# A decoder layer step on one core: norms in steps beside the output projection, shared weight slots, GpSimd stores, outputs fed by the last products

## The chip, the core and the metric

The kernel runs on one core of a Trainium2 chip. TensorE (PE) multiplies, VectorE (DVE), ScalarE (ACT) and GpSimd (POOL) do the elementwise work, and SyncE (SP) issues most DMA transfers; each engine works through its own instructions in order, and a DMA queue through its transfers. The metric is the device time of one execution in microseconds (us).

## What is computed

One layer of a decoder for a prompt of 1024 tokens and 8 sample tokens, 1032 columns in all, with width 1024 and a hidden width of 2816 in both feed-forward networks (FFN):

```python
x = x + 0.5 * swiglu(rms_norm(x, g_ffn1), w1_gate, w1_up, w1_down)
h = rms_norm(x, g_mix)
proj = h @ w_in                     # S5 input, q, k, v, two gates
y_ssm, ... = s5_branch(...)
y_attn, kv_new = dilated_attention_branch(...)
mixed = gate_ssm * (y_ssm @ w_ssm_proj) + gate_attn * (y_attn @ w_attn_proj)
x = x + mixed @ w_o
x = x + 0.5 * swiglu(rms_norm(x, g_ffn2), w2_gate, w2_up, w2_down)
```

## The kernel before

**Arithmetic and tiles.** Every fp32 operand is split in a high part (an ACT cast) and a low part (a DVE subtraction of the cast), and a product is three matmuls: high by high, high by low, low by high. Activations lie with their features on the partitions and the tokens on the free axis, in three chunks of 344. Weights come as 512 KB loads of 128x1024 and are split like the rest.

**Stages.** First FFN (to about 815 us), the mixing stage (`mix`: input projection, S5, attention, gates, `ssm_proj`, to about 1529 us), then at the end of `mix` the join: `attn_proj` of chunks 0 and 1, `wo` of chunk 0, `attn_proj` of chunk 2, `wo` of chunks 1 and 2 (to about 1655 us). `attn_proj` (L1112) multiplies by the gate and adds the other branch; `wo` (L1127) is the output projection, added to the residual in `xT`. Then `wo_norm` (L1152) runs for each of the three chunks: it stores `xT` to the buffer `x_d` in device memory, sums squares (`ss`, L1164), multiplies (`xT`, L1169), and writes the operands of the second FFN (`put`, L1172), which needs sums and differences of chunk 0 and 1 (L1182 to L1187).

**Second FFN.** `ffn_up` (L1244) walks over 22 hidden tiles `f`. Chunks 0 and 1 go through Winograd's form of Strassen's scheme: seven products (`A11*B11`, `S2*T2`, `S3*T3`, `S1*T1`, `A12*B21`, `A22*T4`, `S4*B22`) of 12 matmuls each. Chunk 2 takes four direct ones (`D0`, `D1`) of 12. `wprep` prepares the weights of the next `f` a few steps ahead. `second` (L1262) forms the operands of the down projection from two tiles at a time, splits them into tiles `hs` and stores them to the buffer `hs_d` on SP's queue (55 stores, L1267). `ffn_down` (L1357) runs in three groups of 4, 4 and 3 pairs of hidden tiles. For each group it loads weights (`rd`), loads parts back from `hs_d` (`hload`, L1376), does nine products of four tiles (`run`, L1389, matmuls at L1396), and adds them to accumulators (L1403). In the last group the accumulators are combined (L1443 to L1482), and `out` (L1405) loads the residual `y` from `x_d`, adds it (L1409), transposes on PE (L1415), copies (L1416) and stores (L1420).

**Order and memory.** The order of each engine's instructions comes from the framework's scheduler. SBUF pools are opened and closed like a stack: a tile of a new pool waits for the last reader of what lay in its place. The weight pool `wp` is opened anew for the first FFN and for `mix`; the join uses `wp` too. The second FFN's weights have a pool `wq` of their own, and `ffn_down` has another, `wd`.

## Time and profile before

| | us |
|---|---|
| three timed runs | 2431.59, 2437.26, 2441.64 (median 2437.26) |
| the profiled execution | 2433.45, of which the span of instructions is 2431.7 |
| PE busy | 2308.2 (95%) |
| DVE busy | 1383.5 (57%) |
| ACT busy | 785.0 (32%) |
| POOL busy | 263.4 (11%) |
| mean granted TensorE clock | 0.973 of 2.4 GHz |

A row of the chain of waits is: start, length, engine, tile and line. A row of a table of windows is: the stretch, its length, then for each engine the busy time and (x) the instructions, the granted clock, the share of the DMA engines and GB/s. A row of a table of lines is: line, engine, operation, names, shapes, count, then busy us and mean ns, and idle time ahead with what ended it.

### The profile page before, as it was taken

What the parts mean: (1) busy time and instruction counts of PE and PEld (TensorE: products, weight loads), DVE (VectorE), ACT (ScalarE), POOL (GpSimd) and SP (SyncE); (2) the same over time, 40 slices, a digit from 0 to 9 for tenths busy, and PEclk for the clock granted to TensorE, in tenths of its full rate; (3) what the DMA queues carried; (4) which work ended last, traced back from release to release, by engine and by line L of the source; (5) the groups of instructions that cost most, each with busy time, mean ns of one, the idle gap of its engine ahead of it and who ended that gap; (6) DMA issues with size and microseconds to landing.
All of it is one profiled execution on the core that took longest, in us unless ns stands there. A gap on an engine that the chain in (4) does not pass through costs nothing.

```text
span 2431.7 us, 37109 instructions
## 1 busy us (share of the span) xinstructions
PE 2308.2 (95%) x14409; PEld 2209.9 (91%) x14409; DVE 1383.5 (57%) x2930; ACT 785.0 (32%) x1486; POOL 263.4 (11%) x808
## 2 busy tenths in 40 slices
PE   7999999999999899989999999895999999979996
PEld 6999999999999799978887888894999999979995
DVE  7656544455433734555574535778666666645365
ACT  6211111111112443555444432343333333323121
POOL 3057776000001200000000000000000000000000
PEclk8999999999999899999999999997999999989998
DMA  5333434323232577541331256662333343375453
GB/s 139 96 112 102 126 103 121 112 85 114 90 99 84 159 207 233 164 135 43 96 99 38 73 155 206 185 190 74 112 120 126 113 140 116 128 284 206 161 171 136
DMA packets 306998, 319.44 MB, mean 131 GB/s; under 512 B 30414, under 2 KB 262510, under 8 KB 304262
## 3 DMA queue, kind: packets, MB, share of 16 engines
q1 hardware_dynamic: 302470, 268.86, 35.3%
q10 hardware_dynamic: 2816, 44.00, 6.0%
q0 software_dynamic: 1536, 4.21, 0.5%
q8 instruction: 113, 1.85, 0.3%
q14 instruction: 63, 0.52, 0.1%
HBM read 241.42 MB, written 119.59 MB: 148 GB/s over the span
## 4 chain that ended last, share of the span: by engine, by line
PE 88%; DVE 6%; DMA 4%; ACT 1%; issue 1%; SPq 0%; ACTq 0%; DVEq 0%
PE pm L157 52%; PE pm L1241 18%; PE pm L1396 9%; PE ps L670 2%; PE acc L686 1%; DVE xn L128 1%; PE pT L679 1%; PE pn L969 1%; DMA raw<-in_w_in_dram 1%; DVE wl L143 1%; DMA xr<-in_x_prompt_dram 0%; DMA raw<-in_w_glu_dram 0%; PE pT L809 0%; PE pT L456 0%; DVE al L130 0%
## 5 line engine op out<-in xcount | busy, mean ns | idle before, releaser
L157 PE MATMUL pm<-al,wh 128*128 128x344 f32 x2224 | 709.8, 324 | 2.1 <-DVE rs L1122 1.4
L157 PE MATMUL pm<-ah,wh 128*128 128x344 f32 x2096 | 680.2, 325 | 3.9 <-ACT ah L129 1.9
L157 PE MATMUL pm<-ah,wl 128*128 128x344 f32 x2032 | 656.5, 323 | 0.0
L157 PEld LDWEIGHTS pm<-al,wh 128*128 128x128 f32 x2224 | 418.2, 189 | 10.7 <-issue 4.5
L157 PEld LDWEIGHTS pm<-ah,wh 128*128 128x128 f32 x2096 | 396.3, 189 | 14.6 <-issue 5.6
L157 PEld LDWEIGHTS pm<-ah,wl 128*128 128x128 f32 x2032 | 384.1, 189 | 7.1 <-issue 4.3
L142 ACT CAST wh<-raw 128x1024 fp32r<-128x1024 f32 (+1 forms) x154 | 152.0, 993 | 437.3 <-PE pm L157 384.2
L143 DVE TENSOR_TENSOR wl<-raw,wh 128x1024 fp32r<-128x1024 f32 (+1 forms) x154 | 178.1, 1159 | 161.1 <-ACT wh L142 156.3
L199 DVE SCALAR_TENSOR_TENSOR xT<-pm,xT 128x344 f32<-128x344 f32 x240 | 121.8, 514 | 92.7 <-PE pm L157 92.5
L157 PE MATMUL pm<-hh,wh 128*128 128x344 f32 x528 | 169.8, 322 | 0.0
L157 PE MATMUL pm<-hl,wh 128*128 128x344 f32 x528 | 168.8, 320 | 0.0
L157 PE MATMUL pm<-hh,wl 128*128 128x344 f32 x528 | 168.3, 320 | 0.0
L183 DVE TENSOR_TENSOR h<-h,pm 128x344 f32<-128x344 f32 x66 | 33.7, 511 | 189.5 <-PE pm L157 189.4
L157 PEld LDWEIGHTS pm<-hl,wh 128*128 128x128 f32 x528 | 99.3, 188 | 0.2
L157 PEld LDWEIGHTS pm<-hh,wh 128*128 128x128 f32 x528 | 99.2, 188 | 0.2
L157 PEld LDWEIGHTS pm<-hh,wl 128*128 128x128 f32 x528 | 99.1, 188 | 0.1
L1241 PE MATMUL pm<-ah,wgh 128*128 128x344 f32 x352 | 86.6, 323 | 4.2 <-ACT ah L1149 2.2
L1241 PE MATMUL pm<-al,wgh 128*128 128x344 f32 x352 | 84.9, 322 | 3.3 <-ACT wgh L1149 3.3
L184 ACT CAST hh<-h 128x344 fp32r<-128x344 f32 x66 | 31.5, 478 | 170.1 <-DVE h L183 170.1
L1123 POOL TENSOR_TENSOR rs<-rs,ah 128x344 f32<-128x344 f32 x3 | 2.9, 970 | 600.5 <-DVE rs L1122 600.5
L1241 PEld LDWEIGHTS pm<-ah,wgh 128*128 128x128 f32 x352 | 62.2, 190 | 4.8 <-ACT ah L1149 2.5
L182 ACT ACTIVATE h<-pm 128x344 f32<-128x344 f32 x66 | 30.0, 455 | 112.0 <-PE pm L157 112.0
(469 smaller groups left out, 4540.8 us busy)
## 6 DMA issues: line engine op xcount, KB each, us to landing
out_dram<-in_cache_kv_w_dram ACTq DMA_DIRECT2D x64, 512.0 KB
hs_d<-hs SPq DMA_DIRECT2D x44, 688.0 KB
raw<-in_w_in_dram SPq DMA_DIRECT2D x38, 512.0 KB
e<-hs_d SPq DMA_DIRECT2D x13, 1376.0 KB
raw<-in_w_o_dram SPq DMA_DIRECT2D x24, 512.0 KB
raw<-in_w_gate_dram SPq DMA_DIRECT2D x22, 512.0 KB
raw<-in_w_up_dram SPq DMA_DIRECT2D x22, 512.0 KB
raw<-in_w_down_dram SPq DMA_DIRECT2D x22, 512.0 KB
```

The source lines that it names most:

```text
L128: nc.vector.scalar_tensor_tensor(xn, xT[c][:, k], s.gains[:, z, k:k + 1], r, op0=ALU.mult, op1=ALU.mult)
L142: nc.scalar.copy(h[:, :k], raw[:, :k])
L143: nc.vector.tensor_sub(l[:, :k], raw[:, :k], h[:, :k])
L157: nc.tensor.matmul(p, w[:, kw], a[:, ka], start=first and i == 0, stop=last and i == n - 1)
L182: nc.scalar.activation(h, pg, AF.Silu)
L183: nc.vector.tensor_mul(h, h, pu)
L184: nc.scalar.copy(hh[:, c], h)
L199: nc.vector.scalar_tensor_tensor(xT[c][:, m], p, 0.5, xT[c][:, m], op0=ALU.mult, op1=ALU.add)
L670: nc.tensor.matmul(p[h][:, :nk], qT[hs, s.block(g, b)], kT[hs, ks], start=True, stop=True)
L679: nc.tensor.transpose(pt[:, h, i], sm[:, h, 128 * i:128 * i + 128], s.ident)
L1241: nc.tensor.matmul(p, W[w][:, k], B[:, a, k], start=first and k == 0 and z == 0, stop=k == n - 1 and z == 2, skip_group_check=True)
L1396: nc.tensor.matmul(p[m], W[wz][:, m], t[:, jj, az], start=e == 0 and z == 0, stop=e == n - 1 and z == 2, skip_group_check=True)
```

## The change

It has five parts.

1. `wp` is opened once, for the first FFN and `mix` together. The join moves out of `mix` into a function `join`; its weights and all of the second FFN's come to slots of one pool `wq`: five raw slots `r0` to `r4` and ten split ones `w0` to `w9`, taken by name (`wsl`). A generator `stream` loads the join's weights two ahead. `xT` lies in new pools opened after `mix`.
2. `wo_norm` becomes a generator. `out_norm` runs chunk 0's norm in steps between the column blocks of `wo` of chunk 1, chunk 1's between those of chunk 2, and chunk 2's norm in `ffn_up`, where tile 0's direct products wait until tile 1. Three of the seven additions of squares go to POOL, and the store of `xT` to `x_d` goes to the GpSimd queue.
3. The 55 stores to `hs_d` move from SP's queue to GpSimd's, and so do 23 of the 27 loads from it in `ffn_down`; the first four stay on SP.
4. `ffn_down` takes its weights from the same slots (and six more, `x0` to `x5`, in `wd`), so that its first five loads stand ahead of the end of `ffn_up`.
5. The residual is loaded and added to the accumulators at the end of the second group (`early`, `late`); the last group's products are added straight to outputs (`half`), in a new order, and the last product's four tiles end one after the other and are put out in halves.

The diff, cut:

```diff
+            s.cw = ExitStack()
+            s.wp = pool(s.cw, "wp")
...
-            with ExitStack() as c4:
-                xT, tmp = s.mix(psum, c4)
+            s.mix(psum)
+            s.wq, s.nq = pool(ctx, "wq"), 0
+            psum(ctx, 6, 2)
+            with ExitStack() as c6:
+                hp = pool(c6, "hp2")
+                c2, c01 = ExitStack(), ExitStack()
+                x2, tmp, x01 = pool(c2, "x2"), pool(c2, "tmp2", 2), pool(c01, "x01")
+                xT = [(x2 if c == 2 else x01).tile([128, KT, CH], F32, name=f"xT{c}") for c in range(NCH)]
+                s.join(pool, tmp, xT)
...
+                s.out_norm(tmp, xT)
+                c01.close()
...
+    def join(s, pool, tmp, xT):
+        nc = s.nc
+        for c in range(NCH):
+            nc.sync.dma_start(xT[c], s.x_d[c])
...
+        s.wj = s.stream([(w, 2) for w in wa] * 2 + [(w, 0) for w in wo] + [(w, 2) for w in wa] + [(w, 0) for w in wo] * 2)
...
+            s.attn_proj(tmp, oh, ol, 0)
+            s.attn_proj(tmp, oh, ol, 1)
+            s.wo(xT, 0)
+            s.attn_proj(tmp, oh, ol, 2)
+    def stream(s, srcs):
...
+            raw = s.wq.tile([128, KT, 128], F32, name=f"r{n % 2}")
+            nc.sync.dma_start(raw.rearrange("p (d k) q -> p d (k q)", d=d) if d else raw, src)
...
+            h, l = (s.wq.tile([128, KT, 128], F32R, name=f"w{4 + (2 * n + z) % 6}") for z in range(2))
...
+    def out_norm(s, tmp, xT):
...
+        side.append(s.wo_norm(tmp, xT, 0))
+        s.wo(xT, 1, step)
+        step(99)
+        for _ in range(3):
+            next(s.prep[0])
+        side += [s.wo_norm(tmp, xT, 1)]
+        s.wo(xT, 2, step)
+        for _ in s.prep[0]:
+            step(1)
+        step(99)
+        s.norm2 = s.wo_norm(tmp, xT, 2)
...
-        nc.sync.dma_start(s.x_d[c], xT[c])
+        nc.gpsimd.dma_start(s.x_d[c], xT[c])
...
-                V.tensor_add(ss, ss, sq)
+                (V if k % 2 else nc.gpsimd).tensor_add(ss, ss, sq)
...
-                nc.sync.dma_start(s.hs_d[i:i + n, j].rearrange("i p z n -> p i (z n)"),
-                                  t[:, :n].rearrange("p i z n -> p i (z n)").bitcast(F32))
+                nc.gpsimd.dma_start(s.hs_d[i:i + n, j].rearrange("i p z n -> p i (z n)"),
+                                    t[:, :n].rearrange("p i z n -> p i (z n)").bitcast(F32))
...
         def hload(name, js):
+            q = nc.sync if hn[0] < 4 else nc.gpsimd
+            t = s.slot(('e0', 'e1', 'e2', 'al2')[hn[0] % 4], [128, 4, 2, CH], F32R)
...
+        SETS = {'wa': ('w0', 'w1', 'x0', 'x1'), 'wb': ('w4', 'w5', 'w6', 'w7'), 'ws': ('w2', 'w3', 'w8', 'w9'),
+                'rd': ('r0', 'r1', 'r2', 'r3', 'r4', 'x2', 'x3', 'x4', 'x5')}
...
+        def half(y, x):
+            V.scalar_tensor_tensor(y, x, 0.5, y, op0=ALU.mult, op1=ALU.add)
...
-            y = yo.tile([128, 4, CH], F32, name="y", bufs=1)
-            nc.sync.dma_start(y, s.x_d[c][:, 4 * mh:4 * mh + 4])
-            V.scalar_tensor_tensor(y, x, 0.5, y, op0=ALU.mult, op1=ALU.add)
...
+        def plus(name, c, mh):
+            nc.sync.dma_start(A['x'], s.x_d[c][:, 4 * mh:4 * mh + 4])
+            V.scalar_tensor_tensor(A[name], A[name], 0.5, A['x'], op0=ALU.mult, op1=ALU.add)
+        def early():
+            plus('lo', 2, 0)
...
+        def late():
+            u12('P6', 'P1')
...
+            def ev(m, p):
+                half(A['hi'][:, m], p)
+                if m % 2:
+                    out(2, 1, A['hi'], (m - 1, m))
+            run(two(A21, A22, td), ev, 1)
```

How it moves instructions, at three places. The names are those of the code, with buffer numbers behind.

**SP, at the start of the join.** Loads of the residual (`xT` from `x_d`), of the gates (`rs` from `g_d`, L1108 and L1152 for `ssm_proj`) and of the first projection's weights. Before:

```order
L1059 DMA xT_15754<-x_d 128x2752
L1108 DMA rs_15534<-g_d 128x344
L1059 DMA xT_15755<-x_d 128x2752
L1059 DMA xT_15756<-x_d 128x2752
L137 DMA raw<-in_w_attn_proj_dram 128x2x512
L1108 DMA rs_15550<-g_d 128x344
L1108 DMA rs_15566<-g_d 128x344
```

and in the change, with what each waits for:

```order
L1152 DMA rs_15724<-g_d 128x344 [waits DMAHW2_49,DVE_49]
L1055 DMA xT_15768<-x_d 128x2752 [waits PE_49]
L1055 DMA xT_15769<-x_d 128x2752
L1079 DMA r_15785<-in_w_attn_proj_dram 128x2x512 [waits Activation_49]
L1079 DMA r_15791<-in_w_attn_proj_dram 128x2x512 [waits Activation_49]
```

Before, the weights stood among the gate loads of `ssm_proj`. Now they stand behind all of these and behind two loads of `xT`, the first of which waits for PE; the matmul that it waits for is the last of `ssm_proj`, whose operands lay where `xT` of chunks 0 and 1 now lies.

**DVE, in `wo` of chunk 2 and at its end.** Before, in the stretch behind the last `xT` of `wo` (L1133):

```order
L1169 SCALAR_TENSOR_TENSOR xT_15755<-xT_15755,gains,rs_17020 128x344 x8
L1164 TENSOR_TENSOR ss<-ss,sq 128x344
L1150 TENSOR_TENSOR wgl<-rw,wgh 128x1024
L1150 TENSOR_TENSOR wtl<-S_16921,wth 128x1024
L1220 TENSOR_TENSOR S_17120<-rw 128x512
L1182 TENSOR_TENSOR xT_15754<-xT_15755,xT_15754 128x1376
L1150 TENSOR_TENSOR al_17040<-xT_15755,al_17040 128x1376
```

and in the change, between the `xT` of `wo` (now L1176):

```order
L1217 SCALAR_TENSOR_TENSOR xT_15769<-xT_15769,gains,rs_16823 128x344 x8
L1176 SCALAR_TENSOR_TENSOR xT_15770<-pm,xT_15770 128x344
L1195 TENSOR_TENSOR w_16955<-r_16952,w_16954 128x1024
L1233 TENSOR_TENSOR xT_15768<-xT_15769,xT_15768 128x1376
L1195 TENSOR_TENSOR w_17151<-r_17062,w_17150 128x1024
L1176 SCALAR_TENSOR_TENSOR xT_15770<-pm,xT_15770 128x344
L1195 TENSOR_TENSOR w_17041<-r_16727,w_17040 128x1024
L1195 TENSOR_TENSOR al_16907<-xT_15769,al_16907 128x1376
```

Chunk 1's norm and the first operands come while `wo` of chunk 2 is still on PE.

**PE, at the end of the program.** Before:

```order
L1396 MATMUL pm<-e_23729,wsl 128x344
L1415 MATMUL pT<-ident,y 128x128 x8
L1415 MATMUL pT<-ident,y 88x128 x4
L1415 MATMUL pT<-ident,y 128x128 x8
L1415 MATMUL pT<-ident,y 88x128 x4
L1415 MATMUL pT<-ident,y 128x128 x8
L1415 MATMUL pT<-ident,y 88x128 x4
```

and in the change:

```order
L1522 MATMUL pT<-ident,al_21433 128x128 x2
L1492 MATMUL pm<-e_23483,w_23242 128x344 x3
L1492 MATMUL pm<-e_23481,w_23491 128x344 x3
L1492 MATMUL pm<-e_23483,w_23245 128x344 x3
L1522 MATMUL pT<-ident,al_21433 88x128 x2
L1522 MATMUL pT<-ident,al_21433 128x128 x4
L1522 MATMUL pT<-ident,al_21433 88x128 x2
```

Before, 36 transposes followed the last matmul; now eight do, and the others stand among the matmuls. Listed so, PE has 13928 matmuls and transposes both before and in the change.

## Rows read from the trace of the kernel before

**Rows 1.** The page: busy time of each engine.

```profile
PE 2308.2 (95%) x14409; PEld 2209.9 (91%) x14409; DVE 1383.5 (57%) x2930; ACT 785.0 (32%) x1486; POOL 263.4 (11%) x808
```

**Rows 2.** Windows, from the end of `wo` into `ffn_up`.

```profile
1655.30:1698.80 43.50, 14.06 (x53) 11.76 (x53) 42.38 (x60) 21.91 (x27) 0.00 (x0) 0.67 0.27 81
1698.80:1750.00 51.20, 51.20 (x308) 51.20 (x309) 33.62 (x51) 16.93 (x25) 0.00 (x0) 0.94 0.31 104
1750.00:1800.00 50.00, 50.00 (x319) 50.00 (x318) 33.94 (x49) 18.25 (x27) 0.00 (x0) 1.00 0.35 117
```

**Rows 3.** The chain of waits from 1645 to 1705 us.

```profile
1644.99 9.72 PE pm L157 x62
...
1684.40 1.50 DVE e L1150
...
1698.78 6.30 PE pm L1241 x22
```

**Rows 4.** Lines on DVE from 1650 to 1700 us.

```profile
L1150 DVE TENSOR_TENSOR e<-xT,e 128x1376 fp32r<-128x1376 f32 x3 | 4.7, 1577 | 0.0
...
L1150 DVE TENSOR_TENSOR wgl<-rw,wgh 128x1024 fp32r<-128x1024 f32 x2 | 2.4, 1216 | 0.0
```

**Rows 5.** The chain of waits from 2140 to 2172 us, from `ffn_up` into `ffn_down`.

```profile
2149.42 8.44 DMA hs_d<-hs
...
2159.37 5.13 DMA rd<-in_w_down_dram
...
2165.19 6.87 PE pm L1396 x32
```

**Rows 6.** Windows in `ffn_down`.

```profile
2165.20:2200.00 34.80, 34.80 (x211) 34.77 (x212) 21.29 (x36) 13.90 (x25) 0.00 (x0) 0.95 0.64 240
2200.00:2390.00 190.00, 190.00 (x1223) 189.84 (x1222) 106.39 (x184) 47.90 (x84) 0.00 (x0) 1.00 0.56 193
```

**Rows 7.** The chain of waits at the end, from 2390 us.

```profile
2389.95 8.67 PE pm L1396 x55
...
2423.98 1.13 PE pT L1415 x4
...
2425.74 2.01 DMA out_dram<-xr
...
2427.86 0.58 ACT xr L1416
```

**Rows 8.** Lines on PE from 2398 to 2432 us.

```profile
L1415 PE MATMUL pT<-ident,y 128*128 128x128 f32 (+1 forms) x36 | 8.6, 427 | 19.2 <-DVE y L1409 19.2
```

**Rows 9.** Lines on DVE from 2165 to 2400 us.

```profile
L1150 DVE TENSOR_TENSOR wsl<-S,wsh 128x512 fp32r<-128x512 f32 x44 | 29.4, 684 | 10.5 <-ACT wsh L1149 10.3
L1403 DVE TENSOR_TENSOR ah<-pm,ah 128x344 f32<-128x344 f32 x48 | 22.6, 510 | 15.2 <-PE pm L1396 15.1
```

**Rows 10.** The chain of waits in the join, from 1495 to 1560 us.

```profile
1528.69 1.05 ACT wh L142
...
1532.19 3.44 PE pm L157 x20
...
1541.73 4.28 DMA rs<-g_d
...
1556.04 4.02 PE pm L157 x24
```

**Rows 11.** A window in which `xT` of three chunks is loaded.

```profile
1500.00:1510.00 10.00, 10.00 (x65) 10.00 (x64) 3.38 (x6) 0.62 (x1) 0.00 (x0) 1.00 0.96 368
```

**Rows 12.** DMA issues: what, queue, operation and count, size of one.

```profile
xT<-x_d SPq DMA_DIRECT2D x3, 1376.0 KB
...
raw<-in_w_attn_proj_dram SPq DMA_DIRECT2D x6, 512.0 KB
```

**Rows 13.** The tile `r_d`, the DMA issues of POOL: duration min/median/max in ns.

```profile
L429 POOL DMA_DIRECT2D r_d<-R x16: 594/606/622, 140.2 to 415.4; - x16
...
DMA to landing us min/median/max: 2.3/2.7/6.4
```

More of the change, by code (lines that the diff above doesn't have):

```diff
@@ new lines, in out_norm, with step @@
+    def out_norm(s, tmp, xT):
+        side = []
+        def step(n):
+            for _ in range(n):
+                while side and next(side[0], 0) == 0:
+                    side.pop(0)
+        side.append(s.wo_norm(tmp, xT, 0))
[9 more added lines that the diff above has]
+        s.norm2 = s.wo_norm(tmp, xT, 2)
@@ L1242, in mmk, with ffn_up @@
                                  skip_group_check=True)
-    def ffn_up(s, ap):
+    def ffn_up(s, pool, ctx, first, hp):
         nc = s.nc
@@ L1391, in run @@
             p = [s.pm.tile([128, 512], F32, name="pm")[:, :CH] for _ in range(4)]
             n = len(terms)
-            for e, (W, t, jj) in enumerate(terms):
-                for m in range(4):
-                    for z, (wz, az) in enumerate(((0, 0), (0, 1), (1, 0))):
-                        nc.tensor.matmul(p[m], W[wz][:, m], t[:, jj, az], start=e == 0 and z == 0, stop=e == n - 1 and z == 2,
-                                         skip_group_check=True)
-            acc = A[name]
-            for m in range(4):
+            terms = list(enumerate(terms))
@@ new lines, in run @@
+            for e, m in ([(e, m) for m in range(4) for e in range(n)] if order else [(e, m) for e in range(n) for m in range(4)]):
+                W, t, jj = terms[e][1]
+                for z, (wz, az) in enumerate(((0, 0), (0, 1), (1, 0))):
+                    nc.tensor.matmul(p[m], W[wz][:, m], t[:, jj, az], start=e == 0 and z == 0, stop=e == n - 1 and z == 2,
+                                     skip_group_check=True)
+                if order and e == n - 1:
+                    ev(m, p[m])
@@ new lines, in ops, with two, S, sums @@
+            def ops(z, h, nm):
+                return [wsplit(r[z][:, h], nm, e) for e, r in enumerate(raw)]
+            def two(X, Y, t):
+                return [(W[z], t[z], e) for e, W in enumerate(zip(X, Y)) for z in range(2)]
+            def S(nm, e, f):
+                x = wd.tile([128, 512], F32, name=nm)
+                f(x, raw[e])
+                return x
+            def sums():
+                return [S(f"S{e}", e, lambda x, r: V.tensor_add(x, r[0][:, half1], r[1][:, half1])) for e in range(len(js))]
@@ new lines, in ffn_down, with ev @@
+            p1, u, v = A['P1'], A['P6'], A['P7']
+            A1 = ops(0, half0, "wa")
+            X = sums()
+            run(prod(A1, 'P1', None), lambda m, p: nc.scalar.copy(p1[:, m], p))
+            W = prod(X, 'P5')
+            def ev(m, p):
+                half(A['P3'][:, m], p)
+                half(A['P5'][:, m], p)
+            step(20)
+            run(W, ev)
+            for r, x in zip(raw, X):
+                V.tensor_sub(x, x, r[0][:, half0])
+            W = prod(X, 'P6')
+            def ev(m, p):
+                V.tensor_add(u[:, m], p, p1[:, m])
@@ new lines, in ffn_down, with ev @@
+            run(W, ev)
+            X3 = [S(f"S{3 + e}", e, lambda x, r: V.tensor_sub(x, r[0][:, half0], r[0][:, half1])) for e in range(len(js))]
+            W = prod(X3, 'P7')
+            def ev(m, p):
+                V.tensor_add(v[:, m], p, u[:, m])
+            run(W, ev)
+            half(A['P5'], v)
+            out(1, 1, A['P5'])
+            half(A['P4'], v)
+            A22 = ops(1, half1, "wb")
+            W = prod(A22, 'P4', None)
+            def ev(m, p):
+                half(A['P4'][:, m], p)
@@ new lines, in ffn_down, with ev @@
+            run(W, ev)
+            out(0, 1, A['P4'])
+            for r, x in zip(raw, X):
+                V.tensor_sub(x, r[1][:, half0], x)
+            W = prod(X, 'P3')
+            half(A['P3'], u)
+            def ev(m, p):
+                half(A['P3'][:, m], p)
+            run(W, ev)
+            out(1, 0, A['P3'])
+            A12 = ops(1, half0, "wc")
+            W = prod(A12, 'P2', None)
+            half(A['P2'], p1)
+            def ev(m, p):
+                half(A['P2'][:, m], p)
```

454 lines of the change are left out of this document (252 added, 202 removed).

## The prediction

> **What bounds the kernel now.** The page's first part comes first: PE is busy 95% of the span and every other engine far less [rows 1]. At the full clock a window in mid `ffn_up` holds 319 matmuls in 50 us, so 0.157 us is the price of one [rows 2], and PE's list of work does not shrink. What can be won are stretches in which PE has no work or a low clock. I looked for them in windows and read in the chain of waits what ended each: the norm between `wo` and `ffn_up` [rows 2, 3], the change to `ffn_down` [rows 5], the end [rows 7, 8], and the start of the join [rows 10]. The change touches all four; elsewhere it swaps slots and orders that stand beside PE's work.
>
> **Term 1, norm beside `wo`.** `wo` ends at 1644.99 + 9.72 = 1654.7 [rows 3]. In the next 43.5 us PE does 53 matmuls, 8.3 us of work, at a clock of 0.67, while DVE is busy 42.4 us; in the 51.2 us after that 308 matmuls, 48.4 us of work. So 35.2 + 2.8 = 38 us are lost [rows 2]. The cause is DVE: the operands of chunks 0 and 1 are made by ops of 1.58 us for 1376 columns [rows 4], all behind `wo`. In the change, DVE's rows between chunk 2's first and last residual add in `wo` are 7 weight halves of 1024 columns, 4 ops of 1376, 25 of 344 and 2 of 512. Back to back an op starts some 0.08 us sooner than its mean says (the chain has 1.50 where the mean is 1.577) [rows 3, 4], so that is 7 x 1.14 + 4 x 1.5 + 25 x 0.43 + 2 x 0.60 = 26 us, beside `wo`'s 192 matmuls of 0.157 = 30 us: it fits. What is late next: after `wo`, DVE still has two splits of weights, two sums and two splits of operands ahead of `T2`: 2 x 1.14 + 4 x 1.5 + 0.4 = 8.7 us and its semaphores, some 9.2. PE has three products of 12 matmuls (1.9 us each) in that time and waits about 2.7 us for `T3` and 2.7 us for `T2`: 5 us left over. Chunk 2's norm has until tile 1's direct products, behind some 22 us of PE's work. **Gain 33**; bounds 20 (DVE falls behind by half of its cover, and the clock drops as it does now) and 38 (all of it).
>
> **Term 2, into `ffn_down`.** PE stands from about 2152.1 to 2165.2, and the next 34.8 us hold 211 matmuls, 33.1 us of work [rows 5, 6]: 13.1 + 1.7 = 14.8 us. The chain is an `hs_d` store of 8.44 us and then a weight load of 5.13 us [rows 5]. In the change five weights are in before `ffn_up` ends, and so are two of the parts; 54 matmuls (8.5 us) need nothing else. But `x2` to `x4` lie where `hs` lay and wait for the last stores. Those are issued about 2 us after the last matmul; a landing of 3 to 8.44 us, a load of 3.3 to 5.13 us and a cast of 0.6 us make PE wait 1 to 8 us at `x2`, and DVE splits behind it 1 to 2 us more. I take 5 left. **Gain 10**, bounds 3 and 14.
>
> **Term 3, the end.** The last matmul ends at 2398.6; the span ends at 2431.7: 33.1 us, with 36 transposes [rows 7, 8], each output waiting for its load of `y` and an add. In the change the last product is added straight to the output. From the last transposes on, the chain now takes 2431.7 - 2424.0 = 7.7 us [rows 7], and an add of 0.5 us goes ahead of it [rows 9]: 8.2 us stay. 28 transposes move among the matmuls: at a matmul's price 4.4 us, and at the 0.24 us that they took here at a low clock 6.7 us [rows 8]; I take 5. And DVE gets busier in the last group, where sums and residuals (1376 columns) are added between products. From the end of the second group's eighth product, 227 matmuls (35.6 us) stand beside 35 ops of 512 columns, 24 of 344 and 9 of 1376: 35 x 0.60 + 24 x 0.43 + 9 x 1.5 = 45 us [rows 4, 9]. Some 2 us of that is done ahead; PE waits about 7 us for banks that DVE has not emptied. So 33.1 - 8.2 - 5 - 7 = **gain 13**; bounds 8 (12 us of such waits) and 22 (none, and a shorter chain).
>
> **Term 4, a new wait at the join.** Before, the attention projection's weights landed under `ssm_proj`, and the first matmul came at 1532.2, 3.5 us after the last of `ssm_proj` (1528.7) [rows 10]. Now the load of `xT` of chunk 0 waits for that last matmul, and behind it on SP stand `xT` of chunk 1, the weights, the gates and the second FFN's first weights. 1376 + 1376 + 512 KB [rows 12] at the 368 GB/s that such loads reached [rows 11] are 9.1 us; with an issue of 0.35 us and 1.3 us of latency (2.01 us for a store of 256 KB, less its 0.7 us) [rows 7] the weight lands at +10.8, is cast by +11.9 and split by +13.1: 9 us later than now. Some comes back: from there to `wo` it now takes 23.8 us, with a wait of 4.28 us for a gate load [rows 10] that has landed by then, against 2.4 us of added weight work on DVE. **Loss 7**; bounds 0 (the queue's transfers share the engines, so the small one lands early) and 14 (nothing comes back, and PE's clock is low after the pause).
>
> **The rest: 0.** In `ffn_up` the 55 stores leave SP, and each has until its `hs` slot's next use, two stores on. A load of 1376 KB moved to GpSimd is issued when its buffer's last product ends and needed three products later, 17 to 22 us, against 2.3 to 6.4 us from issue to landing for POOL's stores of 256 KB [rows 13], 3.1 us more for the larger size. At the start of `mix`, weights could be split a few us earlier; I give it nothing.
>
> **Sum.** 2433.45 - 33 - 10 - 13 + 7 = 2384.45, against the profiled execution's own time, 3.8 us under the median of the timed runs, in the middle of their spread. **Forecast 2384 us.** The forecast's own bounds are 2433 - 38 - 14 - 22 + 0 = 2359 and 2433 - 20 - 3 - 8 + 14 = 2416; both ends need all terms to go one way, so I take 2362 to 2412.
>
> **Rivals.**
> - *DVE cannot carry the norm* (chance 0.15). It is busy 98% of the lost stretch [rows 2], and 26 of 30 us beside `wo` leaves little room; a late residual add keeps a PSUM bank, and `wo` itself stalls. Against it: weights are no more work than before. It wins half of term 1: about 2400.
> - *The pools keep their waits* (0.12): `x2` to `x4` come as late as `rd` does now, and the join loses 14: 2384 + 7 + 7 = 2398.
> - *The join's wait is small* (0.12): the weight is not held behind `xT`. Then 2384 - 7 = 2377.
> - *GpSimd's queue is late* (0.04), the one that ends slower. 23 loads of parts and all stores depend on it. Rows speak against it: POOL's issues took 594 to 622 ns, hardly spread [rows 13]. To end at 2450 the 49 us of gain and 12 more must go, 61 us over 23 loads: 2.7 us each beyond the cover of 17 to 22 us, so a landing of over 20 us where the rows bound it by 6.4 + 3.1 = 9.5. Below 17 us it costs nothing.
>
> The Trainium skill, page "SBUF — State Buffer", section "Summary: rules for kernel authors", advises against the fourth part: a transfer issued by GpSimd under DVE work should go to SP's or ACT's queue, because GpSimd's writing of descriptors starves while DVE runs in its fast modes. By that rule this last rival would be the likely one, at 2450 or more. The trace does not agree so far: POOL's 16 issues stayed within 28 ns of each other and landed in 6.4 us at most, though not beside `ffn_down`.
>
> That the change does not do what it says is excluded by the order of instructions.
>
> **How the numbers follow.** The forecast keeps 0.57. Runs of this kernel differ by some 0.4%, so under 0.5%, 12 us, counts as no change: 2425 to 2449. All cases but the last lie under 2425 even with 10 us of bad luck; two of them together with bad bounds reach it. I give faster 0.92, same 0.04, slower 0.04.
>
> **What would show it.** Right: PE's low clock after `wo` shrinks from some 40 us to under 15; the chain at the end of the program has no load of `y` and is under 10 us; POOL's stores land in under 10 us; and SP waits about 10 us of DMA in front of `attn_proj`, at a low clock behind it. Wrong: a gap of PE inside `wo` that ends on DVE, PE waiting on loads issued by POOL, or a tail over 15 us.

## The result and the profile after

| | before | after |
|---|---|---|
| median of the timed runs, us | 2436.32 (2431.59 to 2441.64, 4 runs) | 2407.44 (2401.17 to 2409.23, 4 runs) |
| ratio, with its 95% interval | | 0.9876 [0.9848, 0.9904] |
| span of the profiled execution, us | 2431.7 | 2407.4 |
| mean granted clock | 0.973 | 0.979 |

The change makes the kernel 1.24% faster, 29 us; the forecast of 2384 was 23 us too low, and the range holds the time. The page's first row (to [rows 1]) shows the same work on every engine but POOL:

```profile
PE 2308.5 (96%) x14409; PEld 2212.9 (92%) x14409; DVE 1382.4 (57%) x2921; ACT 789.3 (33%) x1497; POOL 332.2 (14%) x898
```

So the time went where PE waited. Starts and ends of PE's lines in the trace cut the two spans into stretches; every profiled kernel below is cut alike:

| stretch, us | before | after | gain |
|---|---|---|---|
| start to the last matmul of `ssm_proj` | 1528.5 | 1530.7 | -2.2 |
| from there to the first matmul of `wo` | 27.5 | 40.0 | -12.5 |
| `wo` (with `attn_proj` of chunk 2) | 98.5 | 99.8 | -1.3 |
| end of `wo` to end of `ffn_up` | 497.2 | 470.6 | 26.6 |
| end of `ffn_up` to the last product | 247.2 | 260.2 | -13.0 |
| last product to the end | 32.7 | 6.0 | 26.7 |

The first line is no part of the change: in the other twelve profiles of changed kernels it lies between 1525.1 and 1531.8. The last two lines belong together, as the 28 transposes and the residual that left the tail went into the last group.

**Norm to `ffn_up`.** Windows of after (to [rows 2]; columns as there), cut at the end of `wo`, at the end of PE's wait, and behind the return of the clock (it is 0.50 from 1676 to 1686):

```profile
1654.60:1670.60 16.00, 16.00 (x104) 16.00 (x103) 15.73 (x24) 7.97 (x9) 3.46 (x2) 1.00 0.44 129
1670.60:1682.00 11.40, 1.47 (x10) 1.19 (x8) 11.40 (x12) 5.56 (x6) 1.78 (x2) 0.72 0.30 105
1682.00:1690.00 8.00, 8.00 (x38) 7.80 (x39) 7.25 (x7) 2.15 (x3) 0.00 (x0) 0.75 0.50 160
1690.00:1750.00 60.00, 60.00 (x382) 60.00 (x381) 48.53 (x76) 26.17 (x36) 4.17 (x6) 1.00 0.31 103
```

In 19.4 us PE does 48 matmuls, 7.5 us of work at 0.157 us: 11.9 us lost instead of 38. One wait is left, in PE's list of waits (engine, line waited for: us, times, longest), where before had six of 29 us together in this place:

```profile
PE pm L1299 <- ACT e L1194: 9.9, 1, 9.9
```

DVE's timeline there (start, us, line, operation, operands) and one row of POOL's:

```profile
1673.07 0.51 DVE L1176 SCALAR_TENSOR_TENSOR xT<-pm,xT 128x344 f32<-128x344 f32 x1
...
1676.02 1.39 DVE L1286 TENSOR_TENSOR r<-r,r 128x512 f32<-128x512 f32 x1
1677.34 0.50 DVE L1176 SCALAR_TENSOR_TENSOR xT<-pm,xT 128x344 f32<-128x344 f32 x1
...
1680.40 1.58 DVE L1195 TENSOR_TENSOR e<-xT,e 128x1376 fp32r<-128x1376 f32 x1
...
1675.64 1.23 POOL L1209 TENSOR_TENSOR ss<-ss,sq 128x344 f32<-128x344 f32 x1 [6.58 <-DVE ss L1209]
```

`wo` ends on PE at 1670.6; DVE adds its last residual at 1677.34, 6.7 us behind. DVE had not kept up. One sum of 512 columns takes 1.39 us instead of the 0.68 of the one before it, while POOL's addition runs; more of this at the fifth experiment. What moved is chunk 1's norm. Its eight multiplications, before and after:

```profile
1667.13 3.98 DVE L1169 SCALAR_TENSOR_TENSOR xT<-xT,gains,rs 128x344 f32<-128x344 f32 x8
...
1660.09 3.99 DVE L1217 SCALAR_TENSOR_TENSOR xT<-xT,gains,rs 128x344 f32<-128x344 f32 x8
```

They began 12.4 us behind the end of `wo` and now begin 10.6 us ahead of it. Chunk 0's norm did not move: its multiplications begin 42.7 us ahead of the end of `wo` before and 42.2 us ahead after.

**The join.** The chain of waits (start, us, what; to [rows 10]) and two windows, one around the end of the first wait and one ahead of the next:

```profile
1532.00 10.41 DMA r<-in_w_attn_proj_dram
...
1553.78 1.15 DVE w L1195
...
1554.94 3.77 DMA r<-in_w_o_dram
...
1561.11 0.44 DVE al L1169
...
1561.57 3.95 DMA rs<-g_d
```

```profile
1540.00:1550.00 10.00, 6.42 (x24) 6.42 (x25) 4.91 (x6) 3.52 (x4) 0.68 (x1) 0.53 1.07 336
1550.00:1555.00 5.00, 4.72 (x31) 4.44 (x29) 5.00 (x9) 2.76 (x4) 2.21 (x2) 1.00 0.40 128
```

The wait for the first weight is as predicted (10.41 us, then a clock of 0.53), but a weight of `wo` and a gate load hold the chain 3.77 and 3.95 us more. These two loads are issued late, each right behind a DVE operation that the chain names as the one it waited for: the split of a weight, which frees a raw slot, and the last operation on a gate's tile, which frees that.

**Into `ffn_down`.** The chain of after (to [rows 5]):

```profile
2147.47 5.08 DMA hs_d<-hs
...
2153.53 10.34 DMA x<-in_w_down_dram
...
2164.56 7.56 PE pm L1492 x29
```

and, from the timelines of SP, POOL and ACT, the issue of the loads of `x2` to `x5`, that of a part of 1376 KB on GpSimd's queue, and the casts as the weights land:

```profile
2152.61 1.83 SPq L1573 DMA_DIRECT2D x<-in_w_down_dram  x4
2152.72 0.76 POOL L1464 DMA_DIRECT2D e<-hs_d  x1 [4.69 <-PE pm L1492]
2156.13 0.62 ACT L1194 CAST w<-x 128x512 fp32r<-128x512 f32 x1 [7.70 <-DMA x<-in_w_down_dram]
2160.26 0.62 ACT L1194 CAST w<-x 128x512 fp32r<-128x512 f32 x1 [3.52 <-DMA x<-in_w_down_dram]
2163.89 0.62 ACT L1194 CAST w<-x 128x512 fp32r<-128x512 f32 x1 [2.48 <-DMA x<-in_w_down_dram]
```

From 2141.2 to 2200 PE does 275 matmuls, 43.2 us of work in 58.8: 15.6 us lost, no less than the 14.8 before.

**The last group and the end.** Windows in the last group, PE's wait there, and the end of the chain (to [rows 7]):

```profile
2330.00:2340.00 10.00, 8.30 (x52) 7.73 (x50) 10.00 (x14) 2.31 (x5) 1.35 (x2) 1.00 0.78 275
2340.00:2350.00 10.00, 5.46 (x24) 5.47 (x25) 9.94 (x16) 1.66 (x3) 0.00 (x0) 0.66 0.32 88
```

```profile
PE pm L1492 <- DVE ah L1645: 6.1, 1, 6.1
```

```profile
2401.50 0.23 PE pT L1522 x2
...
2401.80 0.38 ACT xr L1523
...
2402.58 1.37 DMA out_dram<-xr
```

In these 20 us PE does 76 matmuls, 11.9 us of work. Of the 8 us lost, 6.1 are one wait for DVE, which is full, and the rest goes by at a low clock behind it. The end is one short chain without a load of `y`.

**GpSimd's queue.** The tile `hs_d` (to [rows 13]; ns min/median/max):

```profile
L1327 POOL DMA_DIRECT2D hs_d<-hs x55: 555/710/739, 1717.9 to 2147.5; - x55
L1464 POOL DMA_DIRECT2D e<-hs_d x18: 743/751/756, 2152.7 to 2360.9; - x18
...
DMA to landing us min/median/max: 2.7/5.0/10.7
```

No issue took over 756 ns beside DVE's work, the stores landed within 7.3 us of their issue and the loads within 10.7, and none of PE's waits in `ffn_down` is for a load that GpSimd issued.

### The profile page after: what moved, and what is told of

Read it like the earlier page. It is cut to its first block, busy times and chain, and to the rows that moved or that the text cites. A ratio compares the mean times of both kernels' runs of the same rounds, so it can differ in the third digit from the quotient of the medians.

```text
span 2407.4 us, 37145 instructions
## 1 busy us (share of the span) xinstructions
PE 2308.5 (96%) x14409; PEld 2212.9 (92%) x14409; DVE 1382.4 (57%) x2921; ACT 789.3 (33%) x1497; POOL 332.2 (14%) x898
## 4 chain that ended last, share of the span: by engine, by line
PE 66%; issue 17%; DVE 7%; DMA 7%; ACT 2%; POOL 1%; SPq 0%; POOLq 0%; ACTq 0%; DVEq 0%
PE pm L157 50%; PE pm L1492 7%; PE ps L670 2%; POOL hs_d L1327 1%; PE pm L1299 1%; DMA r<-in_w_o_dram 1%; DVE w L1195 1%; PE acc L686 1%; PE pT L679 1%; PE pn L971 1%; DMA x<-in_w_down_dram 1%; DMA raw<-in_w_in_dram 1%; DMA num<-s_d 1%; DVE xn L128 0%; ACT w L1194 0%
## 5 line engine op out<-in xcount | busy, mean ns | idle before, releaser
L157 PE MATMUL pm<-ah,wh 128*128 128x344 f32 x1968 | 642.3, 326 | 8.9 <-ACT ah L129 3.8
L157 PE MATMUL pm<-al,wh 128*128 128x344 f32 x1968 | 640.3, 325 | 0.2
L157 PEld LDWEIGHTS pm<-al,wh 128*128 128x128 f32 x1968 | 373.4, 190 | 10.6 <-issue 5.5
L1194 ACT CAST w<-r 128x1024 fp32r<-128x1024 f32 (+1 forms) x134 | 133.7, 999 | 278.7 <-PE pm L1299 172.8
L1299 PE MATMUL pm<-e,w 128*128 128x344 f32 x1056 | 179.4, 320 | 9.9 <-ACT e L1194 9.9
L1195 DVE TENSOR_TENSOR w<-r,w 128x1024 fp32r<-128x1024 f32 (+1 forms) x134 | 156.0, 1164 | 53.5 <-ACT w L1194 53.0
L1299 PE MATMUL pm<-ah,w 128*128 128x344 f32 x1056 | 179.9, 322 | 0.0
L1299 PEld LDWEIGHTS pm<-e,w 128*128 128x128 f32 x1056 | 168.8, 188 | 10.4 <-ACT e L1194 10.2
L1299 PEld LDWEIGHTS pm<-ah,w 128*128 128x128 f32 x1056 | 170.5, 189 | 0.0
L1492 PE MATMUL pm<-e,w 128*128 128x344 f32 x900 | 155.8, 329 | 14.9 <-ACT w L1194 8.1
L1492 PEld LDWEIGHTS pm<-e,w 128*128 128x128 f32 x900 | 147.9, 195 | 16.9 <-ACT w L1194 9.3
L1299 PE MATMUL pm<-al,w 128*128 128x344 f32 x792 | 133.2, 320 | 0.0
```

The source lines that it names most:

```text
L157: nc.tensor.matmul(p, w[:, kw], a[:, ka], start=first and i == 0, stop=last and i == n - 1)
L1194: s.nc.scalar.copy(hi, x)
L1195: s.nc.vector.tensor_sub(lo, x, hi)
L1299: nc.tensor.matmul(p, W[w][:, k], B[:, a, k], start=first and k == 0 and z == 0, stop=k == n - 1 and z == 2, skip_group_check=True)
L1492: nc.tensor.matmul(p[m], W[wz][:, m], t[:, jj, az], start=e == 0 and z == 0, stop=e == n - 1 and z == 2, skip_group_check=True)
```

## The experiments

All are edits of the changed kernel. Three stretches as in the table above, times in us, ratios to the kernel before on the same chip:

| kernel | to `wo` | `wo` to end of `ffn_up` (from the end of `wo`) | `ffn_down` + end | time | ratio [95%] |
|---|---|---|---|---|---|
| after | 40.0 | 470.6 | 260.2 + 6.0 | 2407.44 | 0.9876 [0.9848, 0.9904] |
| 1 weights first | 34.3 | 470.7 | 259.4 + 6.0 | 2404.18 | 0.9876 [0.9862, 0.9891] |
| 2 `hs_d` on SP | 39.9 | 470.5 | 255.9 + 6.2 | 2400.67 | 0.9863 [0.9848, 0.9878] |
| 3 three `hs` | 39.2 | 470.1 | 255.6 + 6.0 | 2404.15 | 0.9880 [0.9863, 0.9896] |
| 4 more steps | 39.8 | 470.1 | 257.5 + 6.0 | 2403.21 | 0.9874 [0.9857, 0.9890] |
| 5 sums on POOL | 39.5 | 472.1 | 271.6 + 6.0 | 2418.69 | 0.9932 [0.9919, 0.9944] |
| 6 four raw slots | 35.0 | 470.3 | 259.9 + 6.0 | 2402.66 | 0.9867 [0.9854, 0.9881] |
| 7 norms after `wo` | 39.9 | 479.1 | 255.3 + 6.0 | 2412.31 | 0.9914 [0.9901, 0.9928] |
| 8 residual late | 39.7 | 470.5 | 252.8 + 8.2 | 2407.71 | 0.9889 [0.9875, 0.9904] |
| 9 loads on SP | 39.8 | 471.6 | 254.9 + 6.1 | 2402.76 | 0.9861 [0.9847, 0.9876] |
| 10 join and `hs_d` | 30.5 | 469.9 | 254.3 + 6.1 | 2392.17 | 0.9815 [0.9800, 0.9829] |
| 11 chunk 2 in order | 40.0 | 470.5 | 255.4 + 6.0 | 2403.36 | 0.9866 [0.9849, 0.9882] |
| 12 weights after | 37.5 | 481.2 | 256.8 + 6.0 | 2414.80 | 0.9915 [0.9901, 0.9930] |

`wo` itself takes 99.1 to 101.8 us in all of them. Two things are seen at once. Times of 2400 to 2408 can't be told apart by the timed runs alone; verdicts on a few us rest on the stretches. And `ffn_down` differs by 5 us between kernels whose edit doesn't touch it (1, 4, 6, 7, 11, 12); the ninth experiment says why.

**1. Weights first.**

```diff
-        for c in range(NCH):
-            nc.sync.dma_start(xT[c], s.x_d[c])
...
             s.attn_proj(tmp, oh, ol, 0)
             s.attn_proj(tmp, oh, ol, 1)
+            for c in range(NCH):
+                nc.sync.dma_start(xT[c], s.x_d[c])
```

> Edit: in the join, the loads of xT are written behind attn_proj of chunks 0 and 1 instead of ahead of the weights. Theory (the weights of attn_proj land late because 2.75 MB of xT stand ahead of them on SP): the first matmul of attn_proj comes about 6 us after the last of ssm_proj instead of 12.6, the stretch from there to wo of chunk 0 shrinks from 39.8 to about 32 us, and the kernel takes about 2400 us. Rival (the loads share the engines, and the waits further on, for the weights of w_o with only two raw slots, set when wo starts): the stretch stays above 37 us, time 2405 to 2408.

`attn_proj` starts 3.4 us after `ssm_proj`, as before the change and 9.5 us earlier than in the change; but `wo` starts only 5.7 us earlier and takes 1.7 us longer. So the stretch lies between the theory's 32 us and the rival's 37. The chain of this kernel shows what took the rest:

```profile
1541.40 8.61 DMA r<-in_w_attn_proj_dram
...
1552.36 3.81 DMA r<-in_w_o_dram
...
1559.08 4.00 DMA rs<-g_d
```

Next in line wait a later weight, a weight of `wo` and a gate. The two loads of `xT` of 1376 KB, issued at 1534.23 here, run ahead of the first of these; the other two waits are as long as in the change (3.77 and 3.95 us), though `xT` has another place. The place in SP's order explains the first wait only. The ratio is that of the change.

**6. The same with four raw slots,** so that the join's weights load further ahead:

```diff
-            raw = s.wq.tile([128, KT, 128], F32, name=f"r{n % 2}")
+            raw = s.wq.tile([128, KT, 128], F32, name=f"r{n % 4 if n < 14 else n % 2}")
```

> Edit: as e1, and the stream of the join's weights uses four raw slots instead of two for its first 14 loads. Theory (with xT out of the way the next wait is for weights of w_o, whose raw slots are still being split): the stretch from ssm_proj's last matmul to wo of chunk 0 goes from 34.3 us in e1 to about 30, time about 2400. Rival (VectorE and the gate loads set it): it stays at 34, time as e1.

`wo` starts at +35.0, no earlier than without the slots. The weights no longer hold the chain, but three gate loads do (6.05, 2.63 and 2.90 us). The first of them falls in 1545:1555, where the DMA engines are full (share 1.14). So the raw slots set the waits for weights, but not the start of `wo`: without those waits gates hold the chain. The second FFN's first two weights, which the change loads at 1536.9 and 1540.2, are not the limit either: they are issued at 1584 and 1588 here.

**7. Norms of chunks 0 and 1 written behind `wo`.**

```diff
-        side.append(s.wo_norm(tmp, xT, 0))
-        s.wo(xT, 1, step)
-        step(99)
+        s.wo(xT, 1)
         for _ in range(3):
             next(s.prep[0])
-        side += [s.wo_norm(tmp, xT, 1)]
-        s.wo(xT, 2, step)
+        s.wo(xT, 2)
+        side += [s.wo_norm(tmp, xT, 0), s.wo_norm(tmp, xT, 1)]
```

> Edit: the norms of chunks 0 and 1 run after the last column block of wo, as in the kernel before; all else as in the change. Theory (of the 24 us of net gain, the norm's steps beside wo bring about 25, and the rest cancels): from the end of wo to the end of ffn_up 497 instead of 470.6 us, time about 2430. Rival (the earlier operands alone, without the steps, bring most of it, since the new pools and slots let ffn_up begin sooner): under 485 us, 2418 or less.

The stretch gets 8.5 us longer, 479.1; before the change it was 497.2. So 18 of its 26.6 us do not hang on where the steps stand in the program, as the rival's number has it. DVE's timeline of this kernel shows one reason:

```profile
1666.36 3.98 DVE L1215 SCALAR_TENSOR_TENSOR xT<-xT,gains,rs 128x344 f32<-128x344 f32 x8
...
1671.89 0.50 DVE L1174 SCALAR_TENSOR_TENSOR xT<-pm,xT 128x344 f32<-128x344 f32 x1
...
1673.82 0.50 DVE L1174 SCALAR_TENSOR_TENSOR xT<-pm,xT 128x344 f32<-128x344 f32 x1
```

Chunk 1's multiplications still run ahead of the last two residuals of `wo`: the scheduler puts them there whatever the program's order. They begin 1.9 us ahead of the end of `wo` (12.4 behind before, 10.6 ahead in the change), so the experiment took back 9 of the 23 us by which the change had moved them. It undid less of the change than its text says, and its 8.5 us are not the worth of the whole move.

**4. Three steps of the norm per block** in `wo` of chunk 2:

```diff
-        s.wo(xT, 2, step)
+        s.wo(xT, 2, lambda n: step(3))
```

> Edit: three steps of the norm per column block of wo of chunk 2 instead of two, the same work. Theory (the order of steps leaves VectorE idle for a third of the first 20 us of that wo and overfills the rest): the operand T3 is ready earlier and PE's wait of 9.9 us for it falls to about 5, time about 2402. Rival (VectorE has too much work in all): the wait moves into wo, no change, 2406 to 2409.

470.1 against 470.6: nothing. But the wait for the operand did fall as the theory says, from 9.9 to 5.0 us:

```profile
PE pm L1299 <- ACT e L1194: 5.0, 1, 5.0
PE pm L1299 <- ACT w L1194: 1.8, 1, 1.8
```

The first `e` is ready 6.2 us behind the end of `wo` instead of 11.3, and PE now waits for weights that DVE splits later. In the first 45 us behind `wo` PE loses 12.2 us here and 12.5 in the change. With DVE full, doing one operand sooner only made another one late.

**11. Chunk 2's norm in program order.**

```diff
         ap, sp = pool(ct, "upt"), None
...
+        step(99)
```

> The whole norm of chunk 2 stands ahead of ffn_up's first tile in the program instead of being drained between its tiles. Theory: of the 26.6 us that the stretch from the end of wo to the end of ffn_up has lost, the steps beside wo bring 8.5, and most of the rest comes from chunk 2's norm being done after the first products; in order, the stretch goes from 470.6 up to 478 or more and the time up by about 8 us. Rival: the rest comes from weights prepared ahead and slots, not from the place of chunk 2's norm; then the stretch stays under 473.

470.5. The rival's number, but the edit hardly does what it was for: chunk 2's multiplications come 26.3 us behind the end of `wo` instead of 27.6, still far behind PE's wait, which ends 11.6 us behind it. What chunk 2's norm would cost ahead of the products stays open.

**12. Tile 0's weights split behind `wo`,** on top of experiment 7:

```diff
-        for _ in range(3):
-            next(s.prep[0])
         s.wo(xT, 2)
         side += [s.wo_norm(tmp, xT, 0), s.wo_norm(tmp, xT, 1)]
-        for _ in s.prep[0]:
-            step(1)
         step(99)
+        s.x2 = xT[2]
+        for _ in s.prep[0]:
+            pass
...
+                if f == 0:
+                    V.tensor_copy(h[0:1, 0, 0:1], s.x2[0:1, 6, 0:1])
                 s.parts(x, h, l)
...
+            if f == 0:
+                V.tensor_copy(S[0:1, 0, 0:1], s.x2[0:1, 6, 0:1])
```

> On top of the kernel with the norms of chunks 0 and 1 written behind wo (2412.31 us; 479.1 us from the end of wo to the end of ffn_up), the splits and sums of tile 0's weights are held back by one-element copies from the last but one residual of wo of chunk 2, so that DVE does them behind wo, as it did in the kernel before. Theory: of the 18 us that this stretch is still shorter there than before, a part comes from weights that are prepared beside wo and the join; four splits of 1.14 us and four sums of 0.6 us are 7 us of DVE work, of which the kernel with the norms behind wo has two splits and two sums (3.5 us) behind wo already; so the stretch gets 3.5 to 7 us longer, 482.5 to 486. Rival: DVE's list up to the first e operand decides alone and holds as many ops of operands and norm as there, so it stays under 481 and the weights bring nothing.

481.2 against 479.1, between the two theories: weights bring some 2 us, not 3.5 to 7. Both kernels have 11.4 to 11.5 us of DVE work between the last residual and the end of the first `e`; ahead of it PE waits for weights in experiment 12 (6.1 and 3.7 us), and once for a sum of squares in experiment 7 (12.1).

What remains of the 18 us no run took apart; it can only be read off the trace of before. There DVE works without a pause from 1657.3 to 1685.9, the end of the first `e`: six operations on operands of 1376 columns (9.0 us), five splits and eight sums of weights (10.6), the rest of chunk 1's norm (6.2), five of chunk 2's squares and the begin of its norm (2.8). That point lies 31.2 us behind the end of `wo` before, 17.5 in experiment 7 and 11.3 in the change. The stretch follows it through these three (497.2, 479.1, 470.6), but not on to experiment 4 (6.2 and 470.1).

**2. Parts stored and loaded by SP.**

```diff
-                nc.gpsimd.dma_start(s.hs_d[i:i + n, j].rearrange("i p z n -> p i (z n)"),
+                nc.sync.dma_start(s.hs_d[i:i + n, j].rearrange("i p z n -> p i (z n)"),
...
-            q = nc.sync if hn[0] < 4 else nc.gpsimd
+            q = nc.sync
```

> Edit: the 55 stores to hs_d and the 23 loads from it go back to SP's queue, all else as in the change. Theory (the queue does not matter, since loads have 17 to 22 us and landings take 2.7 to 10.7): within 4 us of 2407. Rival 1 (GpSimd's queue is late under VectorE's work): faster by 8 us or more, with PE's waits into ffn_down shrinking. Rival 2 (on SP a store that waits for VectorE holds up the weight loads behind it): slower by 5 us or more, with PE waiting in ffn_down on weights.

`ffn_down` takes 255.9 us instead of 260.2. The time lies between the theory (within 4 us of 2407) and the first rival (8 us less), and the ratio cannot be told from the change's. The loads of `x2` to `x4` are issued 11.4 us after `ffn_up` in both, but now land one behind the other, as ACT's casts show:

```profile
2153.36 0.62 ACT L1194 CAST w<-x 128x512 fp32r<-128x512 f32 x1 [7.69 <-DMA x<-in_w_down_dram]
2154.80 0.62 ACT L1194 CAST w<-x 128x512 fp32r<-128x512 f32 x1 [0.82 <-DMA x<-in_w_down_dram]
2156.09 0.62 ACT L1194 CAST w<-x 128x512 fp32r<-128x512 f32 x1
```

**3. Three `hs` tiles** instead of two:

```diff
-                t = sp.tile([128, 2, 2, CH], F32R, name="hs", bufs=2)
+                t = sp.tile([128, 2, 2, CH], F32R, name="hs", bufs=3)
```

> Edit: three hs tiles instead of two. Theory (ScalarE's cast of the last parts waits 6.7 us for the landing of the store that last used its tile, and the loads x2 to x4 wait for the last stores): the x loads are issued some 5 us earlier, PE's waits of 8.1 us on casts of w at the start of ffn_down fall to about 3, time about 2402. Rival (the x loads land 3.6 to 4 us apart whenever they start, and that spacing makes the waits): no more than 2 us, 2405 to 2408.

255.6 us, but not by earlier loads: they are issued at 2152.97, 12 us after `ffn_up`. The last store goes out 4.5 us after `ffn_up` instead of 6.3, but takes 7.23 us to land instead of 5.08. GpSimd's load was issued at 2151.15, ahead of them, and the first of them lands 6.0 us after its issue. A third slot of `hs` does not make the `x` loads start sooner.

**9. Only the loads on SP;** the stores stay with GpSimd:

```diff
-            q = nc.sync if hn[0] < 4 else nc.gpsimd
+            q = nc.sync
```

> All loads of the parts of hs_d and of the residuals are issued by SP; the stores stay with GpSimd. Theory: the change into ffn_down is slow because GpSimd's loads of 1376 KB share the DMA engines with the urgent loads of weights that stood in hs; in one queue they stand behind them. Then the three weight loads land some 1.4 us apart as with everything on SP, instead of 3.6 to 4 us apart; PE's waits for their casts (8.1 us in three in the changed kernel) go to about 3, the stage of ffn_down takes about 256 us instead of 260.2, and the time is some 4 us under the changed kernel. Rival: the stores on GpSimd land late (6.7 us) and that alone sets the wait; then the waits stay at about 8 us and the stage at 260.

254.9 us, and the three weights land 1.3 us apart. So of the second experiment's two halves it is the loads: a load of 1376 KB that nobody needs yet runs beside three of 256 KB that PE waits for. All profiles together show it (times from the first issue of an `x` load):

| kernel | GpSimd's part issued, us | third `x` cast, us | `ffn_down`, us |
|---|---|---|---|
| 6, 1, after | -0.2, 0.0, 0.1 | 11.2, 11.1, 11.3 | 259.9, 259.4, 260.2 |
| 4 | 0.4 | 8.8 | 257.5 |
| 7, 12 | 0.5, 0.5 | 9.0, 8.7 | 255.3, 256.8 |
| 11 | 1.3 | 7.5 | 255.4 |
| 5, with its sums on GpSimd | 0.0 | 11.2 | 271.6 |
| 8, with its residual in the tail | 1.5 | 6.8 | 252.8 |
| 3, with three `hs` | -1.8 | 8.6 | 255.6 |
| 2, 9, 10 | behind, on SP's queue | 6.1 | 255.9, 254.9, 254.3 |

Half a microsecond between two queues goes with 3 to 5 us of `ffn_down`, and in the profiled execution of the change, the slowest of its four (2409.23 us, the fastest 2401.17), it fell badly. How often it does so in executions without a profile is not known. The Trainium skill, page "DMA: Bandwidth & Descriptors", section "Issuing engines are not separate DMA queues", says that transfers of all issuing engines run on the same DMA engines and interleave; this table agrees.

**5. The sums of accumulators on GpSimd** (six additions of 1376 columns, to relieve DVE in the last group):

```diff
-            V.tensor_add(A[x], A[x], A[y])
+            nc.gpsimd.tensor_add(A[x], A[x], A[y])
```

> Edit: the additions of accumulators of 1376 columns (u12) in the last group go from VectorE to GpSimd. Theory (VectorE is over its head between the first products of the last group, and PE's wait of 6.1 us for the add at L1645 comes from it): that wait falls under 2 us and the kernel gains about 5 us, 2402. Rival (at 0.97 us per 344 columns each addition takes 3.9 us on GpSimd, and six of them in a row delay the outputs that need them): PE waits longer there, 2408 or more.

Clearly slower: `ffn_down` takes 271.6 us, 11 more, and the ratio 0.9932 lies outside the change's interval. POOL's and DVE's timelines in the last group:

```profile
2324.74 3.50 POOL L1547 TENSOR_TENSOR ah<-ah 128x1376 f32<-128x1376 f32 x1
...
2328.98 3.14 POOL L1547 TENSOR_TENSOR al<-al,ah 128x1376 f32<-128x1376 f32 x1
```

```profile
2325.13 1.35 DVE L1506 TENSOR_TENSOR al<-pm,al 128x344 f32<-128x344 f32 x3
2326.40 2.38 DVE L1641 TENSOR_TENSOR S<-S,r 128x512 f32<-128x512 f32 x1
2328.70 3.98 DVE L1195 TENSOR_TENSOR w<-S,w 128x512 fp32r<-128x512 f32 x1
```

The three additions from PSUM (`pm`) run at 0.45 us each beside the first addition shown. The operations whose two inputs lie in SBUF do not: 2.38 and 3.98 us for what takes 0.68, ending 0.5 us after POOL's addition does (2328.24 and 2332.12). DVE stands still until POOL's addition ends. The Trainium skill, page "SBUF — State Buffer", section "SBUF: two separate sides", describes such a lock between GpSimd and a DVE operation with two SBUF inputs; the rows agree. It also holds the other way. One of the six additions took 8.28 us, and DVE's operations beside it, nine in a row with two SBUF inputs, took their usual 0.68; POOL's ended after DVE had turned to an addition from PSUM, and the DVE operation behind that one stood in its turn:

```profile
2316.38 8.28 POOL L1547 TENSOR_TENSOR ah<-ah,ah 128x1376 f32<-128x1376 f32 x1 [3.44 <-DVE ah L1506]
...
2321.98 3.22 DVE L1641 TENSOR_TENSOR S<-S,x 128x512 f32<-128x512 f32 x1
```

Six DVE operations stood so, for 16.9 us beyond their usual times, against 9 us of additions that DVE was relieved of. PE's waits in the last group rise from 6.3 to 15.2 us.

**8. The residual of chunk 2 added after the last products,** its second half put out whole:

```diff
-            plus('lo', 2, 0)
-            yield 1
-            plus('hi', 2, 1)
-            yield 1
...
-                half(A['lo'][:, m], p)
+                V.tensor_add(A['lo'][:, m], p, A['lo'][:, m])
...
+            plus('lo', 2, 0)
...
-                half(A['hi'][:, m], p)
-                if m % 2:
-                    out(2, 1, A['hi'], (m - 1, m))
+                V.tensor_add(A['hi'][:, m], p, A['hi'][:, m])
...
-            run(two(A21, A22, td), ev, 1)
+            run(two(A21, A22, td), ev)
+            plus('hi', 2, 1)
+            out(2, 1, A['hi'])
```

> Edit: for chunk 2 alone, whose outputs end last, the residual is added after the products, in one op of 1376 columns for four tiles, and the last output is put out whole. Theory (the tail's gain comes from having no load and no add of four tiles behind the last matmul, and from putting out tile by tile): the time from the last product's matmul to the end goes from 6.0 to 14 us or more, kernel 7 us or more slower than the change. Rival (the load can be early and only the add and twelve transposes remain): about 11 us, 5 us slower.

The end takes 8.2 us instead of 6.0, far from the theory's 14 and the rival's 11, and `ffn_down` with the end 261.0, which is what the kernels with well-placed loads have (261.3 and 261.4 in 7 and 11). The early residual and the output in halves are worth 2.2 us of the tail and no time that can be measured. So the tail's gain must come from the rest of the fifth part: one output is left behind the last product instead of three in series, each with a load of `y` and an add. That is read from the rows of before ([rows 7, 8]); no run took it apart.

**10. The weights first, `xT` of chunks 0 and 1 held back, `hs_d` on SP** (with four raw slots and three `hs`, as in 6 and 3):

```diff
+            nc.sync.dma_start(xT[2], s.x_d[2])
+            for c, m in ((0, 3), (1, 3)):
+                nc.vector.tensor_copy(xT[c][0:1, 0, 0:1], s.ah[c][0:1, m, 0:1].bitcast(F32))
+                nc.sync.dma_start(xT[c], s.x_d[c])
```

> Three edits together: at the join the projection's weights come first and the loads of xT of chunks 0 and 1 are held back by a one-element write until an early output of their attention projection is there, with four raw slots for the first 14 weights; the parts of hs_d go over SP in both directions; hs has three slots. Theory: the join's second wait came from xT's 2.75 MB on the DMA engines beside the weights and gates; held back, wo starts about 28 to 30 us behind ssm_proj's last matmul (40.0 in the changed kernel, 27.5 before, 34.3 with weights first alone), and wo gets no longer than 101.5; with ffn_down at about 256 us the time is 2390 to 2397, some 13 us under the changed kernel. Rival: xT now comes too late for the residual adds in wo, which then waits: wo takes 105 us or more, and the time stays above 2400.

2392.17 us (2387.7 to 2392.98), ratio 0.9815 [0.9800, 0.9829]: faster than both kernels, some 15 us under the change, and the intervals do not meet. `wo` starts at +30.5 and takes 100.8 us, 1.0 more than in the change, so `xT` is not late. The chain of its join holds, besides the first weight, only two gates:

```profile
1528.91 4.02 DMA r<-in_w_attn_proj_dram
...
1544.08 4.63 DMA rs<-g_d
...
1549.70 5.14 DMA rs<-g_d
```

Of the 12.5 us that the join lost, 9.5 come back. The order alone brings 5.7 (experiment 1); the four slots bring none while `xT` runs beside the weights and gates (35.0 in experiment 6); with the same slots and `xT` held back it is 30.5. Whether holding `xT` back does it without the slots was not tried.

## Why the prediction was right and wrong

| term | predicted, us | measured, us |
|---|---|---|
| 1, norm beside `wo` | 33 (20 to 38) | 25.3 (26.6, less 1.3 in `wo`) |
| 2, into `ffn_down` | 10 (3 to 14) | about 0 (15.6 lost against 14.8) |
| 3, the end | 13 (8 to 22) | about 14 |
| 4, the join | -7 (-14 to 0) | -12.5 |
| the rest | 0 | -2.2, which other profiles show to vary so |

**Right.** The place and the sign of terms 1, 3 and 4; the wait of 10 us for the first weight with a low clock behind it; a chain at the end of 6.0 us without `y` (8.2 predicted); 6 to 8 us of waits for DVE in the last group (7 predicted); a clock that is low for some 10 us behind `wo` (under 15 predicted). Term 3 is 26.7 us from the tail, less 8 for DVE and 3 for the transposes, which took 0.11 us each and not the 0.16 to 0.24 of the prediction; 2 us of the difference were not traced. GpSimd's queue, the rival that ends slower, did not come: 55 stores were issued in 555 to 739 ns, and PE waited for none of the loads. The loss that the prediction weighed by the Trainium skill's rule on GpSimd's descriptors (on the third part of the change, which it calls the fourth) is not in these rows. The rule speaks of DVE's fast modes, and no row shows in which mode DVE ran.

The range held by 5 us: terms 1, 2 and 4 all missed the same way, and its upper end was drawn for nearly that.

**Term 1: 7.7 us too much.** The step that failed is "it fits": 26 us of DVE work beside 30 us of PE's. DVE is busy 15.73 of the last 16 us of `wo` and still 6.7 us behind at its end. And "three products of 12 matmuls in that time" was wrong: PE had begun the first of them inside `wo`, did its last 8 matmuls and then stood for 9.9 us at one wait, not 2.7 + 2.7, with a low clock behind it. A part of DVE's lag is POOL's: a sum took 1.39 us beside one of the additions that the change gives to POOL. How much that is in all was not tried. How the gain divides stays open: putting chunk 1's norm back by 9 of 23 us costs 8.5 (experiment 7), and holding the weights' splits back costs 2 more (experiment 12). The rest lies in less DVE work ahead of the first `e`, which was read from the rows, not shown by a run.

**Term 2: nothing came.** Two steps failed. "Issued about 2 us after the last matmul": the last store was issued 6.3 us after it (2147.47 against 2141.2), and the `x` loads 11.4 us. And "a load of 3.3 to 5.13 us" held for one load, not for three beside a part of 1376 KB on another queue: the third was cast 11.3 us after the issue. The part was counted as free because nobody waits for it; what it takes from transfers that someone waits for was not in the sum. In their profiles experiments 2 and 9 have 4 to 5 us less in `ffn_down`; their ratios (0.9863, 0.9861) cannot be told from the change's (0.9876).

**Term 4: 5.5 us too little.** "Some comes back: from there to `wo`" failed. The first matmul came 12.9 us behind `ssm_proj`, much as predicted (13.1; the 9 us later should read 9.6). But from there to `wo` it took 27.1 us, where the prediction's sum is 23.8 - 4.28 + 2.4 = 21.9. The wait of 4.28 us did go, and two others came: a weight of `wo` (3.77 us) and a gate (3.95), each issued only when DVE had freed its place, with the DMA engines at 0.40 in 1550:1555. The sum had a price for the order of the loads and for DVE's work, none for two raw slots, nor for the clock of 0.53 behind the pause, which stood in the bound alone. Taking away the first wait brought 5.7 of its 9.5 us (experiment 1, where the next weight, behind `xT` and two weights of the second FFN, takes 8.61 us). With four slots and `xT` held back it was 9.5 (experiment 10).

**The rivals.** Two were partly true at once: DVE carried three quarters of the norm, and the waits of the pools stayed. Each alone was priced at 2398 to 2400, both in full come to 2414, and the result lies between. That such cases come together was left to the edge of the range.
